# Fetching the sample's matrix-memory state one step sooner, into a third buffer

## The chip, the cores and the metric

The kernel runs on one core of a Trainium2 chip. The metric is the device time of one launch in microseconds (us), the median of several runs. TensorE (PE) does the matrix products, VectorE (DVE), ScalarE (ACT) and GpSimd (POOL) the work on elements, and SyncE (SP) issues most of the transfers (DMA). Each engine works through its own list of instructions in order; a semaphore makes one wait for another.

## The reference

One layer of a streaming encoder runs over 2048 prompt rows and 8 sample groups of 16 rows (128 rows in all), with a model width of 1024:

```python
h   = rms_norm(x)
z   = h @ w_in                               # q, k, v of attention and of the matrix memory, gates
A   = band_attention(...)                    # 8 heads x 64, own chunk and 8 chunks before it
B   = mlstm(...)                             # matrix memory, 4 heads x 128
x   = x + rms_norm(concat(rms_norm(A), sigmoid(o) * head_norm(B)) @ w_out)
x   = x + rms_norm(conv_ffn(rms_norm(x)))    # up, causal convolution of width 3, gated GELU, down
```

The change concerns `B` of the sample rows. Each of the 8 groups has a state of its own, C (128 x 128) and n (128) for each of the 4 heads, which is read, used and written back:

```python
num   = einsum('bhts,bhse->bhte', qk, v) + w_inter[..., None] * einsum('bhtd,bhde->bhte', q, c_prev)
c_new = decay[..., None, None] * c_prev + einsum('bhs,bhsd,bhse->bhde', w_s, k, v)
```

In the kernel n stands as one more column beside C, so a group's state of one head is 128 x 129 numbers.

## The kernel before, in words

All large products are split into three matmuls of rounded operands (high by high, high by low, low by high; lines 95 to 97). The program has two halves. First come the projections by `w_in`, in 28 groups of columns (14 for each half of the rows). Between their matmuls, two streams of small units are interleaved: the attention (`att_stream`) and the matrix memory (`mem_stream`). Each unit is a Python generator that stops (`yield`) with a cost for PE and DVE. After every piece of projection work `pump` (L171) steps one stream or the other while DVE's running cost is behind that of PE; one step (`Pipe.step`, L141) launches one new unit and advances all that are alive. Near the end of this part the output projection `project` (`w_out`, tiles `wo`, L956) takes the projection's place beside the last attention units; its units make their transposes in `mT_pt` from rows `mr`. When its first eight row tiles and the sample's are loaded, `open_ffn` gives the space of the first half to the FFN. There SP loads the normalised rows (`x2r`, L1061), ACT and POOL make their norm, DVE scales them (L1073), and PE transposes them (`h2T_pt`, L1081).

The pieces of one attention unit that matter here are the transposes `pt` of the weights, their rounding into `pth` (ACT, L399) and the rest `ptl` (DVE, L400), the product `ot` with the values (L412, L413), the copy `sh` of half of it (ACT, L418), and, at the end of a group, the transposes `ao`, scaled into `attst` (DVE, L430) and stored to memory (SP, L434).

For the sample rows `mlstm_sample(h)` (L716) yields `own` (the own products of the 16 rows), three empty units, four `batches(bp)` units of two groups each, and `finish`. A `batches` unit loads the states of two groups into `cs` (128 x 258, L763), builds the masked queries `qz` (POOL) and values `vz` (DVE), multiplies `qz` with `cs` and the keys with `vz` (tile `cus`, L775 and L776), updates `cs` (DVE, L779 and L780) and stores it (L781). `cs` shares its buffers (tag `num`) with the tile `num` of the prompt's chunks (L689), in which these collect their result and from which they store it (L649).

What stands in the lists of the engines in the end is set twice. The program text gives the order in which instructions are created, and the framework's scheduler then orders each engine's list by a cost model of its own, in which each instruction has an estimated time. An edit in one place can so change the order of all engines for a long stretch.

Of the kernel before, what the change touches and what calls it, by code (L numbers as in the profile page):

```python
# [10 lines left out]
F32 = mybir.dt.float32  # L11
# [6 lines left out]
P = 128  # L18
# [26 lines left out]
def hymba_step(ctx: ExitStack, tc: tile.TileContext, I: dict, O: dict):  # L45
    nc = tc.nc
# [13 lines left out]
    def ps_sm(name):  # L60
        return psum.tile([P, 512], F32, tag="sm", name=name)
# [4 lines left out]
    def transpose(out, in_, n=P):  # L66
        nc.tensor.transpose(out, in_, ident[:n, :n])
# [60 lines left out]
    pm = p1.enter_context(tc.tile_pool(name="pm", bufs=2))  # L128
# [33 lines left out]
    def bubble():  # L162
        return iter([])
# [319 lines left out]
    def load_gain(h, name):  # L483
        t = pm.tile([P, DH], F32, tag="hgm", name=f"hgm{name}", bufs=1)
        nc.sync.dma_start(t, I["g_mlstm"][0:1, h * DH:(h + 1) * DH].broadcast_to([P, DH]))
        nc.vector.tensor_scalar(t, t, 0.5, None, op0=ALU.mult)
        hgm[h] = t
# [163 lines left out]
    def mlstm(h, half):  # L651
        md, dec, cols = stab[half]
        e = DH + 1

        def load(s):
            sg, o = s.t0 // 4, s.t0 % 4
            s.mb = pm.tile([P, 2, P], F32, tag="mb", name=f"mb{s.nm}", bufs=2)
            nc.sync.dma_start(s.mb, md.rearrange("(c h) t -> h c t", c=8)[h:h + 1, 2 * s.pc:2 * s.pc + 2]
                              .broadcast_to([P, 2, P]))
            yield 0.0, 0.0  # L660
            s.qk = pm.tile([P, 2, 256], F32, tag="mqk", name=f"mqk{s.nm}", bufs=2)
            nc.sync.dma_start(s.qk, qkbd[h][sg][:, :, o * P:o * P + 256])
            vo = pm.tile([P, 2, 2 * DH + 1], F32, tag="mvo", name=f"mvo{s.nm}", bufs=2)
            s.va, s.og = vo[:, :, 0:e], vo[:, :, e:]
            nc.sync.dma_start(vo[:, :, 1:], vobd[h][sg][:, o:o + 2, :])
            nc.gpsimd.memset(vo[:, :, 0:1], 1.0)
            nc.gpsimd.affine_select(out=s.mb, in_=s.mb, pattern=[[0, 2], [1, P]], compare_op=ALU.is_ge, fill=BIG,
                                    base=0, channel_multiplier=-1)
            yield 0.0, 0.0
            if s.pc == 0:  # L670
                load_gain(h, f"{h}_{half}")
            yield 0.0, 0.0

        def chunk(s, c):
            cc = 2 * s.pc + c
            r = cc * HB + h
            col = lambda i: cols[:, i, r:r + 1]
            q_, k_ = s.qk[:, 0, c * P:(c + 1) * P], s.qk[:, 1, c * P:(c + 1) * P]
            sp = ps_sm(f"ms{s.nm}_{c}")
            nc.tensor.matmul(sp[:, 0:P], k_, q_, start=True, stop=True)  # L680
            transpose(sp[:, P:2 * P], k_)
            w = pm.tile([P, P], F32, tag="wexp", name=f"w{s.nm}_{c}", bufs=2)
            nc.scalar.activation(w, s.mb[:, c, :], AF.Exp, bias=col(0), scale=-1.0)
            kw = pm.tile([P, P], F32, tag="kw", name=f"kw{s.nm}_{c}", bufs=2)
            nc.scalar.activation(kw, sp[:, P:2 * P], AF.Identity, scale=col(3))
            nc.vector.tensor_tensor(w, sp[:, 0:P], w, op=ALU.mult)
            yield 0.32, 0.2
            if c == 0:
                s.num = pm.tile([P, 2, e], F32, tag="num", name=f"num{s.nm}", bufs=2)  # L689
            num = s.num  # L690
            acc = ps_sm(f"ma{s.nm}_{c}")
            nc.tensor.matmul(acc[:, e:2 * e], q_, cst[h], start=True, stop=True)
            nc.tensor.matmul(acc[:, 0:e], w, s.va[:, c, :], start=True, stop=True)
            nc.tensor.matmul(acc[:, 2 * e:3 * e], kw, s.va[:, c, :], start=True, stop=True)
            nc.vector.scalar_tensor_tensor(cst[h], cst[h], dec[:, cc, h:h + 1], acc[:, 2 * e:3 * e],
                                           op0=ALU.mult, op1=ALU.add)
            nc.scalar.activation(num[:, c, :], acc[:, e:2 * e], AF.Identity, scale=col(1))
            nc.vector.tensor_tensor(num[:, c, :], num[:, c, :], acc[:, 0:e], op=ALU.add)
            yield 0.65, 0.47
            if c == 0:  # L700
                return
            r0 = 2 * s.pc * HB + h
            sg, o = s.t0 // 4, s.t0 % 4
            finish_heads(num, cols[:, 2, r0:r0 + HB + 1:HB], s.og, h, 2,
                         mixd[sg][:, o:o + 2, 512 + h * DH:512 + (h + 1) * DH], s.nm)
            if half == 1 and s.pc == 3:
                nc.sync.dma_start(O["c_prompt"][h], cst[h])
            yield 0.0, 1.3

        pairs = [SimpleNamespace(pc=pc, t0=8 * half + 2 * pc, nm=f"{h}_{8 * half + 2 * pc}") for pc in range(4)]  # L710
        yield load(pairs[0])
        yield bubble()
        yield bubble()
        for s in pairs:
            if s.pc < 3:
                yield load(pairs[s.pc + 1])  # L716
            yield chunk(s, 0)
            yield chunk(s, 1)

    def mlstm_sample(h):  # L720
        md, dec, cols = stab["s"]
        e = DH + 1
        nm = f"s{h}"
        col = lambda i: cols[:, i, h:h + 1]
        s = SimpleNamespace()
# [31 lines left out]
            yield 0.2, 0.2  # L757

        def batches(bp):
            yield 0.0, 0.0  # L760
            bs = slice(2 * bp, 2 * bp + 2)
            cs = pm.tile([P, 2, e], F32, tag="num", name=f"cs{h}_{bp}", bufs=2)
            nc.sync.dma_start(cs, I["state_c"][h][:, bs])  # L763
            qz = pm.tile([P, 2, P], F32, tag="mqk", name=f"qz{h}_{bp}", bufs=2)
            nc.gpsimd.memset(qz, 0.0)
            for i in range(2):
                c = slice((2 * bp + i) * DS, (2 * bp + i + 1) * DS)
                nc.gpsimd.tensor_copy(qz[:, i, c], s.qt[:, c])
            vz = pm.tile([P, 2, e], F32, tag="mvo", name=f"vz{h}_{bp}", bufs=2)
            nc.vector.tensor_tensor(vz, s.va.unsqueeze(1).broadcast_to([P, 2, e]),  # L770
                                    ind[:, bs].unsqueeze(2).broadcast_to([P, 2, e]), op=ALU.mult)
            yield 0.0, 0.3
            cu = ps_sm(f"cu{nm}_{bp}")
            for i in range(2):
                nc.tensor.matmul(cu[:, 2 * e:3 * e], qz[:, i, :], cs[:, i, :], start=(i == 0), stop=(i == 1))  # L775
            nc.tensor.matmul(cu[:, :2 * e], s.kw, vz.rearrange("p b e -> p (b e)"), start=True, stop=True)  # L776
            nc.vector.scalar_tensor_tensor(s.num[:, 0, :], cu[:, 2 * e:3 * e], col(1), s.num[:, 0, :],
                                           op0=ALU.mult, op1=ALU.add)
            nc.vector.tensor_tensor(cs, cs, dec[:, h, bs].unsqueeze(2).broadcast_to([P, 2, e]), op=ALU.mult)  # L779
            nc.vector.tensor_tensor(cs, cs, cu[:, :2 * e].rearrange("p (b e) -> p b e", b=2), op=ALU.add)  # L780
            nc.sync.dma_start(O["c_sample"][h][:, bs], cs)  # L781
            yield 0.85, 0.8
# [11 lines left out]
        for bp in range(DB // 2):  # L794
            yield batches(bp)
# [390 lines left out]
    for n_, (half, gi) in enumerate(seq):  # L1186
        wh, wl, _ = pend
# [199 lines left out]
    for b, tiles in enumerate(FBLOCKS):  # L1387
# [74 lines left out]
        for f in range(NF):  # L1462
# [7 lines left out]
            e, c = ec[:, 0:512], ec[:, 512:1024]  # L1470
# [38 lines left out]
        for dh in range(2):  # L1509
# [57 lines left out]
            for j in order:  # L1567
                if dh == 0:
                    half, _, ssq = out[j]
# [3 lines left out]
                else:  # L1573
                    half, _, ssq = out[j]
# [104 lines left out]
```

## Time and profile before

| what | us |
|---|---|
| median of 3 runs (lowest and highest 2806.80, 2811.92) | 2807.41 |
| profiled execution, its own time | 2812.18 |
| span from the first to the last instruction of the profiled execution | 2810.5 |
| PE busy | 2729.8 (97%) |
| DVE busy | 1871.9 (67%) |
| ACT busy | 1407.5 (50%) |
| POOL busy | 446.2 (16%) |
| mean granted clock of PE | 0.997 |

The profile is one execution. In its views an instruction has its line, engine, operation, output and inputs (by the program's names, without numbers), and ahead of it in square brackets the time for which its engine was idle and what ended that. A list of waits has the total, the number of times and the longest. A window has the busy time of each engine with its number of instructions, the clock granted to PE (1.00 is full), the busy share of the transfer engines and the GB/s. The chain of waits follows what released each piece of work back in time.

### The profile page before, as it was taken

The numbers are of one execution on the slowest core, as the hardware profiler recorded it, in microseconds if no ns is written. First come the engines' busy times: TensorE is split into PE (matmuls) and PEld (weight loads), VectorE is DVE, ScalarE is ACT, GpSimd is POOL, SyncE is SP. The second block draws the span as 40 slices with busy tenths as digits, with TensorE's granted clock in tenths as the row PEclk, the third lists the DMA queues.
The fourth block names the chain that finished last, engine by engine and source line by source line (L and its number), as shares of the span: only waits on it lengthen the run. The fifth ranks groups of instructions, "written<-read, shape, count | busy, mean of one in ns | idle before, by whom it ended". The sixth has DMA issues, their size and how long they took to land.

```text
span 2810.5 us, 47049 instructions
## 1 busy us (share of the span) xinstructions
PE 2729.8 (97%) x16587; PEld 2550.2 (91%) x16587; DVE 1871.9 (67%) x3442; ACT 1407.5 (50%) x2836; POOL 446.2 (16%) x876
## 2 busy tenths in 40 slices
PE   8899999999999999999999999999999999999998
PEld 7899999998899998878999988799999878999887
DVE  5344455646446678666989886457878854888855
ACT  4345545644356666543545555445555543555533
POOL 1000010211100003244221110011111310222221
PEclk9999999999999999999999999999999999999999
DMA  4544355557555455355645455644544775555585
GB/s 164 170 128 125 111 155 156 177 148 215 164 173 148 141 177 172 106 180 203 199 160 173 162 177 172 218 145 154 157 154 139 266 264 155 171 181 175 188 298 197
DMA packets 313418, 486.04 MB, mean 173 GB/s; under 512 B 55426, under 2 KB 150622, under 8 KB 313054
## 3 DMA queue, kind: packets, MB, share of 16 engines
q1 hardware_dynamic: 274590, 449.21, 50.9%
q10 hardware_dynamic: 38592, 33.83, 3.6%
q8 instruction: 130, 2.13, 0.3%
q14 instruction: 106, 0.87, 0.1%
HBM read 359.36 MB, written 126.70 MB: 173 GB/s over the span
## 4 chain that ended last, share of the span: by engine, by line
PE 51%; DVE 5%; DMA 2%; issue 2%; ACT 1%; POOL 1%; SPq 0%; DVEq 0%; POOLq 0%; ACTq 0%
PE uec L95 5%; PE uec L96 5%; PE uec L97 5%; PE dn L96 4%; PE dn L97 4%; PE dn L95 4%; PE ua L97 3%; PE ua L96 3%; PE ua L95 3%; PE dnm L95 2%; PE dnm L97 2%; PE dnm L96 2%; PE wo L95 1%; PE wo L97 1%; PE wo L96 1%
## 5 line engine op out<-in xcount | busy, mean ns | idle before, releaser
L95 PE MATMUL uec<-B,wuh 128*128 128x384 f32 (+1 forms) x720 | 236.3, 329 | 6.9 <-DVE uu L1492 6.1
L96 PE MATMUL uec<-B,wuh 128*128 128x384 f32 (+1 forms) x720 | 235.2, 327 | 0.0
L97 PE MATMUL uec<-B,wul 128*128 128x384 f32 (+1 forms) x720 | 233.3, 327 | 0.0
L1251 DVE TENSOR_TENSOR gl<-gr,gh 128x768 fp32r<-128x768 f32 (+3 forms) x141 | 118.7, 849 | 163.3 <-ACT gh L1250 163.0
L1250 ACT CAST gh<-gr 128x768 fp32r<-128x768 f32 (+3 forms) x141 | 102.1, 736 | 219.1 <-PE dn L96 194.1
L1250 ACT CAST wuh<-wu 128x512 fp32r<-128x512 f32 x255 | 141.7, 617 | 91.2 <-PE uec L96 87.5
L95 PE MATMUL dn<-wdh,gh 128*128 128x512 f32 x466 | 182.9, 392 | 2.5 <-DVE ug L1403 2.5
L96 PE MATMUL dn<-wdl,gh 128*128 128x512 f32 x466 | 183.9, 395 | 0.0
L97 PE MATMUL dn<-wdh,gl 128*128 128x512 f32 x466 | 168.4, 396 | 0.0
L1251 DVE TENSOR_TENSOR wul<-wu,wuh 128x512 fp32r<-128x512 f32 x255 | 164.3, 683 | 2.8 <-DMA x2d<-mx 2.8
L96 PE MATMUL vo<-wi_l,hT 128*128 128x256 f32 x544 | 155.7, 286 | 0.0
L95 PE MATMUL vo<-wi_h,hT 128*128 128x256 f32 x544 | 154.9, 285 | 0.6 <-DVE mt L199 0.6
L97 PE MATMUL vo<-wi_h,hT 128*128 128x256 f32 x544 | 155.3, 285 | 0.0
L387 DVE CUSTOM_DVE_ANT_0 tmp<-s,nb 128x640 f32<-128x640 f32 (+4 forms) x128 | 94.3, 737 | 77.8 <-PE s L377 74.3
L95 PEld LDWEIGHTS uec<-B,wuh 128*128 128x128 f32 x720 | 135.1, 188 | 11.1 <-DVE uu L1492 8.1
L96 PEld LDWEIGHTS uec<-B,wuh 128*128 128x128 f32 x720 | 135.2, 188 | 0.1
L97 PEld LDWEIGHTS uec<-B,wul 128*128 128x128 f32 x720 | 135.0, 188 | 0.0
L388 ACT ACTIVATE tmp<-tmp,mn 128x640 f32<-128x640 f32 (+4 forms) x128 | 97.6, 762 | 69.9 <-DVE mn L387 65.6
L95 PE MATMUL qk<-hT,wi_h 128*128 128x384 f32 (+1 forms) x384 | 128.6, 335 | 3.5 <-ACT qk_st L226 1.7
L400 DVE TENSOR_TENSOR ptl<-pt,pth 128x640 fp32r<-128x640 f32 (+4 forms) x128 | 93.5, 737 | 55.4 <-ACT pth L399 54.4
L97 PE MATMUL qk<-hT,wi_l 128*128 128x384 f32 (+1 forms) x384 | 128.0, 333 | 0.0
L96 PE MATMUL qk<-hT,wi_h 128*128 128x384 f32 (+1 forms) x384 | 127.8, 333 | 0.0
(409 smaller groups left out, 8886.6 us busy)
## 6 DMA issues: line engine op xcount, KB each, us to landing
wu<-in_w_up SPq DMA_DIRECT2D x220, 256.0 KB, 4.0
wu<-wsd SPq DMA_DIRECT2D x176, 256.0 KB, 3.7
wdr<-in_w_down SPq DMA_DIRECT2D x132, 256.0 KB, 5.4
gr<-gd SPq DMA_DIRECT2D x78, 384.0 KB, 3.9
wi_raw<-in_w_in SPq DMA_DIRECT2D x52, 512.0 KB, 4.3
wsd<-ws SPq DMA_DIRECT2D x88, 256.0 KB, 4.0
gd<-g SPq DMA_DIRECT2D x44, 384.0 KB, 2.7
kraw<-kTd SPq DMA_DIRECT2D x112, 128.0 KB, 3.2
```

Of the source, the lines that this page charges most:

```text
L95: nc.tensor.matmul(out, ah, bh, start=start, stop=False, skip_group_check=onto)
L96: nc.tensor.matmul(out, ah, bl, start=False, stop=False, skip_group_check=onto)
L97: nc.tensor.matmul(out, al, bh, start=False, stop=stop, skip_group_check=onto)
L387: nc.vector.tensor_tensor_reduce(o_, s_, b_, 1.0, 3e38, ALU.add, ALU.min, accum_out=mn)
L388: nc.scalar.activation(tmp[:, :n], tmp[:, :n], AF.Exp, bias=mn, scale=-1.0, accum_out=rsum[:, i % 4, hh:hh + 1])
L400: nc.vector.tensor_tensor(s.ptl[:, sl, qc], ptv, s.pth[:, sl, qc], op=ALU.subtract)
L1250: nc.scalar.copy(h, r)
L1251: nc.vector.tensor_tensor(l, r, h, op=ALU.subtract)
```

## The change

The tag `num` has three buffers in place of two (in both places that use it, since the third is one of the tag), and in `batches` the tile `cs` is taken and its load issued ahead of the first `yield`, that is when the unit is launched, and no longer in the next step of the stream. The number of instructions that compute, store or load is the same, and so is what is computed. The third buffer takes 1032 bytes in each partition.

```diff
@@ -686,7 +686,7 @@
             if c == 0:
-                s.num = pm.tile([P, 2, e], F32, tag="num", name=f"num{s.nm}", bufs=2)
+                s.num = pm.tile([P, 2, e], F32, tag="num", name=f"num{s.nm}", bufs=3)
@@ -757,10 +757,10 @@
         def batches(bp):
+            bs = slice(2 * bp, 2 * bp + 2)
+            cs = pm.tile([P, 2, e], F32, tag="num", name=f"cs{h}_{bp}", bufs=3)
+            nc.sync.dma_start(cs, I["state_c"][h][:, bs])
             yield 0.0, 0.0
-            bs = slice(2 * bp, 2 * bp + 2)
-            cs = pm.tile([P, 2, e], F32, tag="num", name=f"cs{h}_{bp}", bufs=2)
-            nc.sync.dma_start(cs, I["state_c"][h][:, bs])
             qz = pm.tile([P, 2, P], F32, tag="mqk", name=f"qz{h}_{bp}", bufs=2)
```

The lists of all five engines differ from about 410 us to about 1230 us of the run before, and are alike ahead of and behind that. Three places show how. In the first, SP's list where the first head's states are loaded, `num_4` and `num_6` are the prompt's results in the same buffers, `mvos` the values of the sample rows, and the numbers behind `cs` are the unit and a running number. A row with + is of the change, one with - of the kernel before:

```order
 L319 DMA nb_0_4597<-relrow 128x640
+L762 DMA cs_0_4895<-in_state_c 128x258
 L649 DMA mixd_163<-num_4_4477 128x2x128
 L736 DMA mvos_4767<-vobd_4_146 128x256
-L763 DMA cs_0_4923<-in_state_c 128x258
+L762 DMA cs_1_4925<-in_state_c 128x258
 L485 DMA hgm_0_5398<-in_g_mlstm 128x128
 L649 DMA mixd_163<-num_6_4571 128x2x128
 L328 DMA qraw_0_4463<-qTd_0_109 64x512 x2
 L331 DMA kraw_0_0_4464<-kTd_0_90 64x512 x2
-L763 DMA cs_1_4974<-in_state_c 128x258
+L762 DMA cs_2_4968<-in_state_c 128x258
```

The first load moved ahead of the store of `num_4` (whose data is in another buffer now), and each of the next two stands where its predecessor stood. The second place is SP's list in the last head, the kernel before first:

```order
L649 DMA mixd_163<-num_6_7763 128x2x128
L763 DMA cs_1_8072<-in_state_c 128x258
L905 DMA atts_171<-so_8945 128x512
L891 DMA svr_1_9078<-in_cache_v 128x512
L891 DMA svr_2_9118<-in_cache_v 128x512
L781 DMA out_c_sample<-cs_0_8032 128x258
L763 DMA cs_2_8117<-in_state_c 128x258
L891 DMA svr_3_9140<-in_cache_v 128x512
L891 DMA svr_4_9167<-vs 16x512
L781 DMA out_c_sample<-cs_1_8072 128x258
L763 DMA cs_3_8164<-in_state_c 128x258
```

and with the change:

```order
L762 DMA cs_1_8034<-in_state_c 128x258
L1155 DMA wi_raw_8888<-in_w_in 128x1024
L485 DMA hgm_1_10431<-in_g_mlstm 128x128
L649 DMA mixd_163<-num_6_7763 128x2x128
L1155 DMA wi_raw_9116<-in_w_in 128x1024
L762 DMA cs_2_8066<-in_state_c 128x258
L781 DMA out_c_sample<-cs_0_8001 128x258
L762 DMA cs_3_8111<-in_state_c 128x258
```

`cs_2` no longer stands behind a store of `cs`; `cs_3` stands behind that of `cs_0` in place of that of `cs_1`. Loads of other streams (`svr`, the sample attention's cached values; `wi_raw`, projection weights) have changed places with them. The third place is the start of the FFN on PE: the last attention transposes `ao`, the output projection `wo` behind them, and the first FFN transposes `h2T_pt`, the kernel before first. Where the line of dots stands, 46 more `wo` matmuls follow, so that there are 51 of them:

```order
L67 MATMUL ao_3_15152<-ident,attT_3_14865 128x128 x2
L95 MATMUL wo_1_15191<-wo_13608,mt_14889 128x512
L96 MATMUL wo_1_15191<-wo_13608,mt_14889 128x512
L97 MATMUL wo_1_15191<-wo_13608,mt_14889 128x512
L95 MATMUL wo_0_15255<-wo_13395,mt_15099 128x512
...
L97 MATMUL wo_1_15332<-wo_13608,mt_15099 128x512
L1081 MATMUL h2T_pt_0_0_15268<-ident,x2r_15187 128x128 x4
```

and with the change, where the dots stand for 19 and there are 24:

```order
L67 MATMUL ao_3_15152<-ident,attT_3_14865 128x128 x2
L96 MATMUL wo_0_15255<-wo_13608,mt_15099 128x512
L97 MATMUL wo_0_15255<-wo_13608,mt_15099 128x512
L97 MATMUL wo_1_15332<-wo_13395,mt_15099 128x512
L95 MATMUL wo_1_15332<-wo_13395,mt_15099 128x512
...
L97 MATMUL wo_1_15332<-wo_13608,mt_15099 128x512
L1081 MATMUL h2T_pt_0_0_15268<-ident,x2r_15187 128x128 x4
L1081 MATMUL h2T_pt_1_0_15289<-ident,x2r_15189 128x128 x4
L1081 MATMUL h2T_pt_1_1_15316<-ident,x2r_15189 128x128 x4
L67 MATMUL mT_pt_15303<-ident,mr_15185 128x128 x8
L67 MATMUL mT_pt_15435<-ident,mr_15314 128x128 x8
```

27 of these `wo` now stand ahead of `ao`, and two groups of `mT_pt` stand together. On SP, `attst`, one load of a norm's gain and the loads of `x2r` follow each other in both kernels.

## The prediction

> **What bounds the kernel now.** I read the page first. Its busy line and its chain say which engine the end hangs on:
>
> ```profile
> span 2810.5 us, 47049 instructions
> PE 2729.8 (97%) x16587; PEld 2550.2 (91%) x16587; DVE 1871.9 (67%) x3442; ACT 1407.5 (50%) x2836; POOL 446.2 (16%) x876
> PE 51%; DVE 5%; DMA 2%; issue 2%; ACT 1%; POOL 1%; SPq 0%; DVEq 0%; POOLq 0%; ACTq 0%
> ```
>
> TensorE (PE) is busy for 97% of the span. The change adds and removes no matmul, so two things can move the time: the 2810.5 - 2729.8 = 80.7 us in which PE idles, and the clock that it is granted. Everything below is therefore a sum over PE's waits. The second view is the list of waits of PE; these are the rows that concern the stretch where the orders differ:
>
> ```profile
> PE cus L775 <- DMA cs<-in_state_c: 8.4, 6, 2.5
> PE mT_pt L67 <- DVE mr L979: 3.0, 1, 3.0
> PE pt L67 <- DVE ptl L400: 1.8, 1, 1.8
> PE h2T_pt L1081 <- DVE x2r L1073: 1.6, 1, 1.6
> ```
>
> The first row is the change's target: of the 16 groups of `cus` matmuls, 6 waited for the load of their state, 8.4 us in all, 2.5 us at most. The tile's own view and SyncE's (SP's) waits between 400 and 760 us show why the loads are late:
>
> ```profile
> L763 SPq DMA_DIRECT2D cs<-in_state_c x16: 327/332/520, 410.0 to 719.5; - x16
> SPq L763 <- DMA out_c_sample<-cs: 21.4, 7, 4.5
> SPq L763 <- DMA mixd<-num: 11.3, 7, 2.8
> ```
>
> The queue held 14 of the 16 loads back until a store out of the wanted buffer had landed: 7 times the store of an earlier `cs`, 7 times that of a `num`. One worst case, from the timeline, SP's and PE's rows:
>
> ```profile
> 703.87 0.61 PE L775 MATMUL cus<-cs,qz 128*128 128x129 f32 x4
> 709.74 0.34 SPq L781 DMA_DIRECT2D out_c_sample<-cs  x1
> 714.30 0.33 SPq L763 DMA_DIRECT2D cs<-in_state_c  x1
> 716.48 0.68 PE L775 MATMUL cus<-cs,qz 128*128 128x129 f32 x4 [2.46 <-DMA cs<-in_state_c]
> ```
>
> Unit 0 multiplies at 703.87, its result is stored at 709.74, the load into that buffer leaves at 714.30, unit 2 starts at 716.48. From `cus` of one unit to `cus` of the unit that inherits its buffer this chain takes 716.48 - 703.87 = 12.6 us.
>
> **The change, part by part.**
>
> *The waits that it removes: -8.4 us.* The load is issued one pump step sooner, and a third buffer makes that possible. By the order on SP, `cs_0` now stands ahead of the store of `num_4`, `cs_1` and `cs_2` each behind a `num` store, and only `cs_3` behind the store of `cs_0`; before, both `cs_2` and `cs_3` stood behind a `cs` store. A load lands within a few us of its issue (714.30 to 716.48 above is 2.2 us), and by the new order 24 to 28 matmuls lie between two units, 3.2 us or more at the shorter price worked out below, so I take units 0 to 2 as free. Bounds: 0 (nothing gained) to 8.4.
>
> *The clock that goes with the longest wait: -1.7 us.* Windows; the columns are the stretch, its length, busy time of PE, PEld, DVE, ACT, POOL, the granted clock, the DMA share and GB/s:
>
> ```profile
> 709.00:716.40 7.40, 4.67 (x32) 4.44 (x32) 3.51 (x10) 1.53 (x3) 0.64 (x3) 1.00 0.50 142
> 716.50:720.50 4.00, 4.00 (x19) 3.81 (x20) 2.35 (x10) 0.83 (x2) 0.64 (x3) 0.57 0.54 165
> 653.80:657.80 4.00, 3.97 (x33) 3.93 (x34) 2.47 (x11) 2.61 (x9) 0.88 (x4) 1.00 0.59 185
> ```
>
> Behind the wait of 2.46 us PE ran 4.0 us at 0.57, which is 4.0 x 0.43 = 1.7 us of lost work; behind the wait of 2.14 us at 653.8 it stayed at 1.00. If the long wait goes, so does this loss.
> [...]
>
> *What stays of the waits: +1.0 us.* `cs_3` still needs the chain of 12.6 us, from `cs_0`'s matmuls on. By the new order 93, 81, 80 and 74 matmuls lie between the two in the four heads (before, between 55 and 83 lay in such a chain). The price of one, from two windows:
>
> ```profile
> 590.00:600.00 10.00, 10.00 (x76) 10.00 (x75) 4.60 (x16) 4.74 (x16) 1.80 (x5) 1.00 0.53 160
> 703.00:712.00 9.00, 8.22 (x50) 7.45 (x51) 4.62 (x12) 1.16 (x2) 1.63 (x7) 1.00 0.61 180
> ```
>
> 10.00 / 76 = 0.132 us in the first, 8.22 / 50 = 0.164 in the second. At 0.164 they take 15.3, 13.3, 13.1 and 12.1 us: only the last falls short, by 0.5. At 0.132 they take 12.3, 10.7, 10.6 and 9.8, short by 0.3, 1.9, 2.0 and 2.8, which is 7.0. I take 1.0, near the first, because the stretches around `cus` are the ones that the second row measures; the ends are 0 and 7.0.
>
> *What the moved order costs at the end of the attention phase: +6.3 us.* The scheduler has put all engines in another order between some 410 and 1230 us. The memory units come 7 to 14 us of PE work sooner, the attention's last units up to 17 us later, the w_out projection (`wo`) 7 to 9 us sooner. That matters in one place. After the last attention transposes (`ao`), SP must store `attst` before it may load `x2r`, from which the FFN's first transposes (`h2T_pt`) are made. PE, SP, ACT and DVE in the timeline, the transfer from the chain of waits:
>
> ```profile
> 1207.18 0.38 PE L67 MATMUL ao<-ident,attT 128*128 128x128 f32 x2
> 1207.60 0.69 DVE L430 TENSOR_TENSOR attst<-ao,rinv 128x512 f32<-128x512 f32 x1 [1.91 <-PE ao L67]
> 1208.31 0.57 SPq L434 DMA_DIRECT2D mixd<-attst  x1
> 1210.08 7.15 DMA x2r<-x2d
> 1218.07 1.28 DVE L1073 SCALAR_TENSOR_TENSOR x2r<-x2r,n_rs,g 128x1024 f32<-128x1024 f32 x1 [3.45 <-POOL n_rs L84]
> 1219.51 0.63 PE L1081 MATMUL h2T_pt<-ident,x2r 128*128 128x128 f32 x4
> 1221.74 1.06 PE L1081 MATMUL h2T_pt<-ident,x2r 128*128 128x128 f32 x8 [1.61 <-DVE x2r L1073]
> ```
>
> `ao` to `h2T_pt` is 1219.51 - 1207.18 = 12.33 us, and the order on SP after `ao` is the same in both kernels. What covers it are `wo` matmuls:
>
> ```profile
> 1207.50:1219.50 12.00, 11.95 (x51) 9.27 (x50) 1.38 (x2) 0.00 (x0) 1.00 0.57 169
> ```
>
> (the same kind of window, of `wo` alone). 51 of them take 11.95 us, 0.234 each, and leave no wait and no slack. In the new order 24 stand there. The other 27, 27 x 0.234 = 6.3 us, were done earlier, and PE waits as long for `h2T_pt`: 12.33 - 0.38 - 24 x 0.234 = 6.3. The page's issues of transfers (KB of one, us to landing) bound it from below:
>
> ```profile
> x2r<-x2d SPq DMA_DIRECT2D x17, 512.0 KB, 3.9
> ```
>
> If 7.15 shrinks to 3.9, the hole is 6.3 - 3.2 = 3.1 us. From above I take 7.0, the 0.63 us of the first `h2T_pt` once more: after such a wait they may run at about half the clock. I expect that to cost 0, because the next wait (1.61 us, for DVE) covers it.
>
> *The transposes behind it: 0.* `mT_pt` of the next but one tile now stands directly behind that of the next one, where before some 30 `wo` lay between. DVE's rows there:
>
> ```profile
> 1221.51 1.28 DVE L1020 SCALAR_TENSOR_TENSOR mx<-mx,n_rs,norm_row 128x1024 f32<-128x1024 f32 x1
> 1222.71 0.68 DVE L1008 COPY mx<-wo 128x512 f32<-128x512 f32 x1
> 1223.31 2.49 DVE L979 TENSOR_SCALAR mr<-mr,att_rs 128x512 f32<-128x512 f32 x1
> 1231.84 0.48 DVE L979 TENSOR_SCALAR mr<-mr,att_rs 128x512 f32<-128x512 f32 x1
> ```
>
> The copy of 0.68 us is out of this chain now (its `wo` are done early), and L979 took 2.49 us once and 0.48 once; the second `mT_pt` adds one L1020, one L1094 (0.68) and one L979 to the path. If the first L979 becomes the short one, 1.5 us are gained; if both are long, 2.0 are lost. I take 0.
>
> *The transposes before it: +1.6 us.* The last pair of attention units now has no `wo` between the transposes `pt_15` and the product `ot_14`, where 23 stood. Then PE waits for the cast on ACT (L399), the copy ahead of it in ACT's queue (L418) and DVE's difference (L400):
>
> ```profile
> L399 ACT CAST pth<-pt 128x640 fp32r<-128x640 f32 x96 | 65.5, 692 | 41.1 <-PE pt L67 29.1 <-PE ot L412 7.9 <-DMA qkbd<-qb_st 2.1
> L418 ACT COPY sh<-ot 64x256 f32<-64x256 f32 x64 | 23.6, 369 | 40.2 <-PE ot L413 38.8 <-ACT va_st L224 0.4
> L400 DVE TENSOR_TENSOR ptl<-pt,pth 128x640 fp32r<-128x640 f32 (+4 forms) x128 | 93.5, 737 | 55.4 <-ACT pth L399 54.4
> ```
>
> Two casts and the copy are 2 x 0.69 + 0.37 = 1.75, of which a little lies under `pt_15` itself; the wait of 1.8 us on `ptl` in the list above is the same pattern. Bounds 0.7 (one cast) to 2.5 (two casts, the copy and a difference of 0.74).
>
> *Other waits in the reordered stretch: 0.* PE idled
>
> ```profile
> 760.00:1060.00 300.00, 298.89 (x2281) 293.64 (x2279) 184.34 (x419) 185.10 (x443) 19.44 (x61) 1.00 0.56 166
> 1060.00:1207.00 147.00, 143.21 (x840) 123.43 (x841) 108.86 (x213) 80.74 (x207) 44.19 (x65) 1.00 0.42 128
> ```
>
> 1.1 us and 3.8 us in these stages. They can vanish at best, so -4.9, and I allow as much on the other side.
>
> The sum: -8.4 - 1.7 + 1.0 + 6.3 + 0 + 1.6 + 0 = -1.2 us. The profiled execution took 2812.18 us, 1.7 more than its span, so it would be 2811.0. It lies 4.8 us above the median of the runs shown (2807.41), so the forecast for the median is 2806.2. I count less than 0.2% (5.6 us) as no change, since a measurement of this kernel can hardly tell less; -1.2 is the same.
>
> **The rivals.**
>
> *The hole stays small, and the gain stays.* The 27 `wo` are not lost: they stand where PE idled 3.8 us, and if they fill that and the `x2r` loads take 3.9 us, the terms are -8.4 - 1.7 + 1.0 + 3.1 + 1.6 - 3.8 = -8.2: 2799.2. For it: 7.15 us is the landing of several loads at once, in a busy stretch. Against it: SP's rows after `ao` are unchanged, and so is what is in flight there.
>
> *The wait moves to `cs_3`.* It is slower than before. Place: the fourth unit of each head, behind the store of the first. Price: 7.0 in place of 1.0, and 1.7 of clock, once, for the wait of 2.8. It decides from the point where PE takes less than 12.6 / 80 = 0.158 us for a matmul between the two. -1.2 + 6.0 + 1.7 = +6.5: 2813.9. For it: the window at 590 has 0.132. Against it: the one at 703 has 0.164.
>
> *The change doesn't do what it says.* SP is one queue; `cs_0` now stands behind the loads of the attention's caches, and if SP is late at them the load lands no sooner. Then the 8.4 and 1.7 stay and only the moved order counts: +6.3 + 1.6 = +7.9: 2815.3. For it: SP waited 21.4 + 11.3 us at these loads. Against it: those waits were for buffers, of which there is one more.
>
> **How the numbers follow.** Forecast (same) 0.50, gain with a small hole 0.25, wait at `cs_3` 0.15, no earlier load 0.10. The terms left open put 0.03 of the forecast's half beyond 5.6 us on either side; the fast rival ends faster in nine tenths of its cases (0.23), the two slow ones slower in eight tenths (0.20). That gives faster 0.26, slower 0.23, same 0.51. The range leaves out a tenth at either end: from 2798, just under the fast rival's value, to 2816, just above the slowest. The forecast's own range is 2802 to 2812: 4 below, if the hole stays at 3.1 and a wait in the tail is filled, 6 above, if `cs_3` costs its 7.0.
>
> **What would show it.** Right: no `cus` wait on a load beyond the fourth unit of a head, clock 1.00 in that stretch; PE waits some 6 us for `x2r` ahead of the first `h2T_pt`, with 24 `wo` after `ao`; a wait on `ptl` or `pth` before the last `ot`. Wrong: `cus` waits still of several us (second or third rival), a wait of under 4 us for `h2T_pt` (first), or a new PE wait of over 3 us between 760 and 1200 us that none of the terms names.

## The result and the profile after

The change is slower. Its median is 2834.39 us (2832.77 to 2835.34, 4 runs) against 2809.66 us for the kernel before (2806.8 to 2814.83, 4 runs): a ratio of 1.0089, with a 95% interval of 1.0075 to 1.0102. The forecast was no change, 2806.2 us in a range from 2798 to 2816. The page of the change (profiled execution 2832.77 us):

```profile
span 2831.0 us, 47052 instructions
PE 2739.9 (97%) x16587; PEld 2556.9 (90%) x16587; DVE 1873.2 (66%) x3442; ACT 1408.3 (50%) x2836; POOL 444.3 (16%) x876
```

The span grew by 20.5 us. Half of that, 91.1 - 80.7 = 10.4 us, is idle time of PE; the other half, 10.1 us, is PE working longer at the same 16587 matmuls. The list of PE's waits says that the change's target was met, and what grew:

```profile
PE mT_pt L67 <- DVE mr L979: 10.3, 6, 4.6
PE h2T_pt L1081 <- DVE x2r L1073: 7.4, 2, 6.2
PE ss L95 <- ACT skh L846: 4.0, 2, 3.1
PE wo L95 <- ACT wo L946: 2.1, 1, 2.1
PE cus L776 <- DVE vz L770: 1.9, 1, 1.9
PE cus L775 <- DMA cs<-in_state_c: 1.5, 1, 1.5
PE ot L412 <- ACT pth L399: 1.3, 1, 1.3
```

`cus` waited 8.4 us for its loads before and waits 1.5 now; `mT_pt` went from 3.0 to 10.3 and `h2T_pt` from 1.6 to 7.4. Where in the program that lies is best seen in windows between the same instructions of both kernels. The five stages are: from 152 us, where both kernels are alike, over the sample's memory to the first `qb` matmul of the second half of the rows (757.4 us before); from there to the first `wo`; to the last `ao`; to the first `h2T_pt`; to the first FFN up-projection. The columns are as in the prediction's windows. Before:

```profile
152.00:757.40 605.40, 586.61 (x4156) 568.75 (x4155) 319.02 (x815) 296.52 (x723) 62.11 (x190) 1.00 0.51 153
757.40:1055.50 298.10, 297.05 (x2274) 292.82 (x2273) 181.97 (x414) 182.23 (x438) 18.22 (x58) 1.00 0.55 162
1055.50:1207.20 151.70, 147.85 (x865) 126.95 (x864) 113.30 (x221) 85.24 (x218) 45.41 (x67) 1.00 0.44 135
1207.20:1219.50 12.30, 12.25 (x54) 9.60 (x53) 3.45 (x5) 4.36 (x10) 1.79 (x4) 1.00 0.58 175
1219.50:1329.10 109.60, 104.37 (x496) 84.78 (x497) 75.46 (x75) 41.72 (x87) 52.55 (x62) 0.98 0.58 193
```

and with the change:

```profile
151.40:757.30 605.90, 587.73 (x4156) 570.11 (x4155) 318.94 (x815) 295.81 (x723) 60.54 (x190) 0.99 0.50 153
757.30:1048.70 291.40, 290.57 (x2216) 286.35 (x2215) 170.74 (x385) 173.24 (x412) 15.18 (x51) 1.00 0.52 157
1048.70:1226.10 177.40, 166.89 (x950) 141.71 (x949) 124.87 (x251) 96.25 (x245) 47.22 (x75) 0.98 0.41 131
1226.10:1238.30 12.20, 6.00 (x27) 4.54 (x25) 3.37 (x5) 4.64 (x11) 1.73 (x4) 0.89 0.42 150
1238.30:1351.50 113.20, 106.29 (x496) 86.81 (x497) 74.41 (x72) 41.09 (x85) 52.44 (x63) 0.94 0.56 187
```

The second number of a row is its length, the third PE's busy time, and their difference the idle time. Three things are to be seen.

- In the first stage, the one that the change is about, nothing was gained: 18.8 us idle before, 18.2 after, although the waits on the loads are gone.
- In the second stage 58 matmuls fewer are done (2216 for 2274), and in the third 85 more (950 for 865). The attention's and memory's units have slid from the second stage into the third, and 27 `wo` have come into it from the fourth.
- The third stage has 10.5 us idle where it had 3.9, the fourth 6.2 for 0.05, the fifth 6.9 for 5.2. (Outside the five stages, where the lists are alike, PE idled 3.2 us less in this execution, so that the sum is 10.4.) In the third stage 8.3 of the 10.5 us are waits of the output projection itself: `mT_pt` for its rows `mr` 4.9, in four waits, and `wo` for the cast of its weights (ACT, L946) 2.1 and for its rows `mt` 1.3. In the old order these were 0.4 there, and the longest wait was 1.8, of `pt` for `ptl`.

Most of the rest is the clock. Four stretches of the change at half clock, by windows:

```profile
740.70:747.50 6.80, 6.80 (x22) 5.27 (x21) 2.89 (x5) 2.10 (x5) 1.23 (x2) 0.50 0.51 175
1058.20:1061.60 3.40, 3.40 (x11) 2.61 (x10) 3.40 (x9) 3.40 (x8) 0.00 (x0) 0.50 0.84 300
1146.90:1150.30 3.40, 3.40 (x16) 3.36 (x16) 3.08 (x10) 3.13 (x9) 0.19 (x1) 0.50 0.59 231
1235.70:1252.70 17.00, 7.82 (x33) 6.66 (x34) 13.52 (x11) 7.53 (x15) 12.36 (x14) 0.50 0.48 154
```

By the granted 0.50 I put half of the busy time in them, (6.8 + 3.4 + 3.4 + 7.8) / 2 = 10.7 us, as lost; in the kernel before the same sum between 400 and 1300 us is 3.2 (3.4 us at 717.1 and 3.0 busy at 1225.7, both at 0.50). That is an estimate, and a little high: in the change's trace `wo` matmuls of one shape start 0.43 us apart at 0.50 (from 1058.58 to 1060.71) and 0.23 at 1.00 (from 1227.04 to 1230.31). By the estimate 7.5 us of the 10.1 are clock. The other 2.6 us stay unplaced.

The end of the attention phase, PE's timeline in the change:

```profile
1226.12 0.38 PE L67 MATMUL ao<-ident,attT 128*128 128x128 f32 x2
1238.33 1.12 PE L1081 MATMUL h2T_pt<-ident,x2r 128*128 128x128 f32 x4 [6.23 <-DVE x2r L1073]
1240.66 1.94 PE L1081 MATMUL h2T_pt<-ident,x2r 128*128 128x128 f32 x8 [1.21 <-DVE x2r L1073]
1243.32 1.97 PE L67 MATMUL mT_pt<-ident,mr 128*128 128x128 f32 x8 [0.71 <-DVE mr L979]
1249.90 1.97 PE L67 MATMUL mT_pt<-ident,mr 128*128 128x128 f32 x8 [4.62 <-DVE mr L979]
```

The hole ahead of `h2T_pt` is there and is 6.23 us long, 12.21 after `ao`. But the last `ao` itself is already 18.9 us later than before (1226.12 for 1207.18), of which 27 x 0.234 = 6.3 are the `wo` done ahead of it. So some 12.6 us were lost before this place, for which the prediction had 1.6 us of transposes and otherwise nothing. The wait of 4.62 us for the second `mT_pt` is long because DVE's two instructions ahead of it took 5.4 us, and both ran beside POOL's two additions (timeline, DVE and POOL):

```profile
1244.53 2.83 DVE L1094 TENSOR_TENSOR B<-b,B 128x512 fp32r<-128x512 f32 x1
1247.29 2.56 DVE L979 TENSOR_SCALAR mr<-mr,att_rs 128x512 f32<-128x512 f32 x1
1243.74 5.82 POOL L1021 TENSOR_TENSOR mx<-mx 128x1024 f32<-128x1024 f32 x2
```

L1094 took 0.68 us and L979 0.48 where no such addition ran (the change at 1254.62 and 1011.73). In the traces of the kernel before and of the change, L979 took 0.47 to 0.49 us in all 8 cases without one of these additions (L1021) beside it, and 2.49 to 2.65 in 25 of the 26 with one.

### The profile page after: what moved, and what is told of

Read it like the earlier page. It is cut to its first block, busy times and chain, and to the rows that moved or that the text cites. A ratio compares the mean times of both kernels' runs of the same rounds, so it can differ in the third digit from the quotient of the medians.

```text
span 2831.0 us, 47052 instructions
## 1 busy us (share of the span) xinstructions
PE 2739.9 (97%) x16587; PEld 2556.9 (90%) x16587; DVE 1873.2 (66%) x3442; ACT 1408.3 (50%) x2836; POOL 444.3 (16%) x876
## 4 chain that ended last, share of the span: by engine, by line
PE 76%; DMA 10%; DVE 7%; ACT 3%; issue 3%; POOL 1%; SPq 0%; ACTq 0%; DVEq 0%; POOLq 0%
PE uec L95 5%; PE uec L96 5%; PE uec L97 5%; PE dn L96 4%; PE dn L97 4%; PE dn L95 4%; PE ua L97 3%; PE ua L96 3%; PE ua L95 2%; PE dnm L95 2%; PE dnm L97 2%; PE dnm L96 2%; PE qb L97 2%; PE qb L95 2%; PE qb L96 2%
## 5 line engine op out<-in xcount | busy, mean ns | idle before, releaser
L95 PEld LDWEIGHTS uec<-B,wuh 128*128 128x128 f32 x720 | 135.3, 188 | 10.5 <-DVE uu L1492 7.0
```

The source lines that it names most:

```text
L95: nc.tensor.matmul(out, ah, bh, start=start, stop=False, skip_group_check=onto)
```

## The experiments

All ratios are to the kernel before, run on the same chip beside them. Theory A says that the third buffer makes the scheduler put the engines in another order, and that this order costs the time. Theory B says that fetching sooner, or a third buffer as such, costs it, whatever the order.

**The load alone.** The load ahead of the first `yield`, but with two buffers (the diff is to the change):

```diff
-                s.num = pm.tile([P, 2, e], F32, tag="num", name=f"num{s.nm}", bufs=3)
+                s.num = pm.tile([P, 2, e], F32, tag="num", name=f"num{s.nm}", bufs=2)
-            cs = pm.tile([P, 2, e], F32, tag="num", name=f"cs{h}_{bp}", bufs=3)
+            cs = pm.tile([P, 2, e], F32, tag="num", name=f"cs{h}_{bp}", bufs=2)
```

> The load issued ahead of the first yield as in the change, but with two buffers. The lists of all five engines come out in the order of the kernel before. Theory A (the third buffer lets the scheduler put the engines in another order, and that order costs the time; the earlier place of the load in the text does nothing by itself): ratio to before 1.000, within 0.2%. Theory B (fetching sooner collides with other transfers or blocks SP, whatever the order): slower, towards 1.009.

Measured: 0.9998 (0.9987 to 1.0008; 2809.66 us). Moving the load in the text does nothing: with two buffers the scheduler puts it where it stood. Since the lists are those of the kernel before, this run is also a second look at it, and two of its numbers matter: the `cus` waits on loads were 3.4 us (3 of them) in place of 8.4 (6), and the first stage, the sample's, had 604.1 - 589.4 = 14.7 us idle in place of 18.8:

```profile
150.30:754.40 604.10, 589.38 (x4156) 571.08 (x4156) 319.55 (x815) 296.02 (x723) 64.01 (x190) 0.99 0.50 153
```

**The buffer alone.** Three buffers in both places, the load where it was:

```diff
-            cs = pm.tile([P, 2, e], F32, tag="num", name=f"cs{h}_{bp}", bufs=2)
+            cs = pm.tile([P, 2, e], F32, tag="num", name=f"cs{h}_{bp}", bufs=3)
```

(and the same for `num`; the diff is to the kernel before.)

> Three buffers, the load where it was. The lists come out in the order of the change. Theory A: as the change, 1.009 (1.007 to 1.011). Theory B, if the step sooner is what costs: 1.000; if it is the third buffer as such, 1.009 too, which the kernel with a third buffer and the old tail (x02) then tells apart.

Measured: 1.0068 (1.0051 to 1.0084; 2829.16 us), which overlaps the change's 1.0075 to 1.0102. Its waits are the change's; the last row is its sample stage:

```profile
PE mT_pt L67 <- DVE mr L979: 10.6, 6, 4.6
PE h2T_pt L1081 <- DVE x2r L1073: 6.9, 2, 5.7
PE cus L775 <- DMA cs<-in_state_c: 0.3, 1, 0.3
150.50:752.90 602.40, 588.10 (x4156) 570.55 (x4156) 318.97 (x815) 296.21 (x723) 60.44 (x190) 0.99 0.51 154
```

So of the two edits the buffer is the whole change. Its sample stage had 602.4 - 588.1 = 14.3 us idle, as much as the 14.7 of the run before, though `cus` waited 0.3 us in place of 3.4. Three kernels further down have the change's lists in this stage too, and they had 14.6, 17.1 and 17.4 us. So one order's idle time differs by some 4 us from one execution to the next (14.7 and 18.8 with the old order, 14.3 to 18.2 with the new one), and a gain of 8.4 isn't among these numbers.

**A third buffer with the old order behind it.**

```diff
-            cs = pm.tile([P, 2, e], F32, tag="num", name=f"cs{h}_{bp}", bufs=2)
+            cs = pm.tile([P, 2, e], F32, tag="csx" if bp in (0, 2) else "num", name=f"cs{h}_{bp}", bufs=1 if bp in (0, 2) else 2)
```

> cs_0 and cs_2 share one buffer of their own, cs_1, cs_3 and num keep the two of num: three buffers in all. Only cs_2 still waits for a store of cs (that of cs_0). The engines' order differs from before up to some 725 us and is the old one from there: 51 wo behind the last ao. Theory A: the cus waits fall from 8.4 to 2 to 4 us and nothing is lost later: 0.998 (0.9965 to 1.000), no wait of 6 us for h2T_pt. Theory B (a third buffer or an earlier load costs as such): slower by 0.3% or more.

Measured: 1.0000 (0.9991 to 1.0010; 2810.98 us). Theory B falls: a third buffer with earlier loads is there, and nothing is lost. But the gain that A expected isn't there either. The `cus` wait fell to 2.0 us as expected, and the sample stage had 604.2 - 589.5 = 14.7 us idle, like the repeat of the old order:

```profile
152.70:756.90 604.20, 589.50 (x4156) 571.10 (x4155) 318.81 (x815) 296.06 (x723) 61.78 (x190) 0.99 0.51 153
```

**One buffer given to one unit.** The same edit with `bp in (1,)`, and in a second kernel with `bp in (3,)`:

> Two buffers of num as before, and one buffer of its own for cs_1 of every head; the load where it was. cs_1 is fetched a head ahead, cs_0, cs_2 and cs_3 as late as before. PE's order is that of the change (apart from a few transposes at the start), with 24 wo behind the last ao. Theory A (the order costs the time): as the change, 1.007 to 1.009, with the same waits at mT_pt and h2T_pt. Theory B (a third buffer or an earlier load costs as such): as the next kernel, since both give one buffer to one unit.

> The same with the buffer given to cs_3 in place of cs_1. PE's order is that of before from some 725 us on, with 51 wo behind the last ao. Theory A: 1.000 (0.998 to 1.001), waits at mT_pt and h2T_pt as before. Theory B: as the kernel with a buffer for cs_1.

Measured: 1.0099 (1.0083 to 1.0115; 2835.18 us) with the buffer for `cs_1`, and 1.0016 (1.0005 to 1.0027; 2812.18 us) with the buffer for `cs_3`. The two give the same memory to one unit each and fetch one unit early; they differ in the order that the scheduler made of it. The waits, `cs_1` first:

```profile
PE mT_pt L67 <- DVE mr L979: 9.3, 6, 4.6
PE h2T_pt L1081 <- DVE x2r L1073: 7.2, 2, 6.0
```

```profile
PE mT_pt L67 <- DVE mr L979: 3.0, 1, 3.0
PE h2T_pt L1081 <- DVE x2r L1073: 1.2, 1, 1.2
```

This is theory A's case. The second is slightly above the bound given (1.001).

**Only the hole undone.** The change, with the sample tile's `wo` bound behind the last `ao` (`last_ao` holds that instruction; the bond is one of issue order on PE):

```diff
-                    mm3(acc, s.mt[:, 0, k, :], s.mt[:, 1, k, :], wo[k][0][:, c], wo[k][1][:, c],
-                        start=(k == 0), stop=(k == KT - 1))
+                    with tc.issue_after(last_ao[0].ins) if t == SAMPLE else ExitStack():
+                        mm3(acc, s.mt[:, 0, k, :], s.mt[:, 1, k, :], wo[k][0][:, c], wo[k][1][:, c],
+                            start=(k == 0), stop=(k == KT - 1))
```

> The change, with the 48 wo matmuls of the sample's row tile bound to be issued behind the last ao. PE's order differs from the change in 13 rows, so all is as in the change but the hole. If the hole before h2T_pt and the half clock behind it are the whole loss: back to before or below, 0.997 to 1.000. If they are a part, as the change's trace says (wait 6.2 to about 1, second mT_pt wait 4.6 to 0, clock 2.4 us): 10 us less than the change, 1.005, and the waits between 1050 and 1226 us stay. If the order at that place doesn't matter: 1.009.

Measured: 1.0053 (1.0039 to 1.0068; 2826.54 us), as expected for "a part". Third, fourth and fifth stage of it:

```profile
1047.40:1219.50 172.10, 160.13 (x929) 135.91 (x927) 125.07 (x251) 96.25 (x245) 47.19 (x75) 0.99 0.43 135
1219.50:1231.60 12.10, 11.46 (x51) 8.92 (x49) 2.77 (x4) 2.66 (x5) 0.93 (x3) 1.00 0.50 156
1231.60:1343.90 112.30, 107.13 (x496) 86.85 (x497) 73.26 (x75) 42.76 (x91) 51.49 (x63) 0.95 0.56 189
```

The hole is closed (12.1 - 11.5 = 0.6 us idle), and the third stage still has 12.0 us of idle time. The hole is less than half of the loss.

**The third stage: memory units beside `wo`?** One wait of the change, in its chain of waits, suggested a cause:

```profile
1135.66 3.76 DMA mb<-md
1139.48 0.41 POOL mb L667
1139.89 0.69 POOL mf L641
1140.60 0.62 DVE num L647 x2
1141.21 1.20 DVE mx L1020
1143.15 2.59 DVE mr L979
1145.79 0.66 PE mT_pt L67 x4
```

POOL waits for the load of a memory unit (`mb`), DVE behind it makes that unit's end (`num`) and only then the row norm `mr`, and PE's `mT_pt` comes last. In the order before, the last memory units are further on when `wo` begins. So on top of the hole's bond, each `wo` of the first eight row tiles was bound behind the memory matmuls ahead of it in the text (`last_ms` holds the last of these):

```diff
-                    with tc.issue_after(last_ao[0].ins) if t == SAMPLE else ExitStack():
+                    with tc.issue_after(last_ao[0].ins) if t == SAMPLE else tc.issue_after(last_ms[0].ins) if t < 8 else ExitStack():
```

> The change, with the sample tile's wo behind the last ao as in the kernel with 48 wo there, and besides each wo of the prompt's first eight row tiles bound to be issued behind the memory matmuls that are ahead of it in the program text, so that the last memory units no longer stand beside wo. If the waits between 1050 and 1226 us (idle of PE 10 to 12 us there, 3.6 to 3.9 in the old order) come from the memory's work on POOL and DVE getting in the way of the row norms: idle there falls to some 5 us, and the time to some 1.002 to 1.003. If they come from the crowding of the attention's tail alone: no change against 1.005.

Measured: 1.0105 (1.0089 to 1.0122; 2837.23 us): slower, and neither expectation came in. Its second and third stage:

```profile
757.50:1086.00 328.50, 311.96 (x2323) 304.12 (x2322) 194.67 (x443) 195.53 (x466) 18.95 (x61) 0.98 0.51 155
1086.00:1236.40 150.40, 143.86 (x820) 122.58 (x818) 100.40 (x192) 71.61 (x189) 43.56 (x64) 1.00 0.38 117
```

The idle time of the third stage fell to 6.5 us, near the 5 foreseen, but the second now has 16.5, most of it in waits of attention units behind the last projection matmul (`s` for `ptl` 4.1 us, `pt` for `mn` 3.2). I read this as: the streams' units wait wherever they stand without projection work between them, and moving `wo` moves the place. So the question was no longer what is beside `wo`, but why units that needed filler were left over when the projection ended.

**The projection held behind the streams.** From the lists of PE one can count how many projection and `wo` matmuls stand ahead of the first matmul of a unit (`s4_8` is the scores of attention head 4, row tile 8; `ms3_8` memory head 3):

| unit | before | change | projection held |
|---|---|---|---|
| `s0_8` | 3636 | +0 | +0 |
| `s2_8` | 4048 | +20 | +5 |
| `s3_12` | 4367 | +29 | +1 |
| `s4_8` | 4456 | +50 | +8 |
| `s4_12` | 4637 | +91 | +19 |
| `s5_12` | 4752 | +69 | 0 |
| `ms3_8` | 4848 | +63 | 0 |
| last `ao` | 5112 | +24 | 0 |

In the second half of the rows the change lets the projection run ahead of the streams, by up to 91 matmuls. The last experiment takes that back and leaves all else of the change, its loads and its order up to some 800 us, as it is. A table names, for 41 tiles of the projection and of `wo` from `s0_8` on, the scores that stand ahead of them in the old order:

```diff
+    HELD = {
+        "vo0_1_12": "s0_9", "vo0_1_14": "s0_10", "vo0_1_15": "s0_11", "qb1_1_0_1": "s1_9", "qb1_1_0_2":
...
+        "s6_11", "wo3_0": "s7_9", "wo4_0": "s7_11", "wo7_0": "s7_15"
+    }
+
+    def held(name):
+        ctx_ = ExitStack()
+        for n in HELD.get(name, "").split():
+            ctx_.enter_context(tc.issue_after(mark[n].ins))
+        return ctx_
...
+                    with held(f"{name}_{t}") if k == 0 else ExitStack():
```

(the last line around the first product of each tile, in the places where projections are made; `mark` holds a matmul of each unit's scores. The sample's `wo` stay bound behind the last `ao`.)

> The change, with the projection's and the output projection's matmuls of the second half bound behind the attention scores that stand ahead of them in the order of before (41 such bonds; the sample's wo behind the last ao). In the change the attention's and memory's units of the second half fall behind the projection by 20 projection matmuls at the second pair, 50 at the fourth, 90 at the fifth, and still 50 to 70 when w_out begins; here by 0 to 25 and then 0. The first 800 us keep the change's order and its early loads. Theory A as it stands now (the loss is that the streams fall behind, so that 70 matmuls which fill waits are used up before the attention's tail): ratio 0.998 to 1.001, idle of PE between the first wo and the last ao back from 10 to 4 us, h2T_pt without the wait of 6 us, half clock as in the old order. If the loss comes from the third buffer, the earlier loads or the order of the first 800 us: 1.005 or more stays.

Measured: 1.0014 (1.0002 to 1.0025; 2813.49 us), a little over the bound of 1.001. The five stages:

```profile
151.60:759.40 607.80, 590.45 (x4157) 572.05 (x4156) 319.48 (x815) 296.21 (x723) 60.58 (x190) 0.99 0.50 153
759.40:1057.80 298.40, 296.65 (x2275) 292.66 (x2273) 182.93 (x414) 184.02 (x440) 19.19 (x57) 1.00 0.53 162
1057.80:1209.80 152.00, 147.73 (x864) 127.09 (x864) 112.67 (x222) 84.51 (x215) 45.32 (x68) 1.00 0.42 134
1209.80:1221.80 12.00, 12.00 (x55) 9.62 (x53) 3.46 (x5) 4.33 (x10) 2.24 (x6) 1.00 0.51 184
1221.80:1330.80 109.00, 104.16 (x498) 84.75 (x497) 75.42 (x75) 41.72 (x87) 52.39 (x61) 0.98 0.58 194
```

From the second stage on they are the stages of the kernel before (298.4, 152.0, 12.0 and 109.0 us for 298.1, 151.7, 12.3 and 109.6). So the loss of 0.9% is the order of the second half, nearly all of it, and neither the buffer nor the loads. The third stage agrees over all kernels: it idled 10.4 to 12.0 us in the four that have the change's order there, and 3.3 to 4.3 in the five that have the old one. What is shown is that this order costs it. That the cost arises because filler (projection matmuls that stand between units that wait) is used up too early is how the table, the stages and the run with `wo` behind the memory fit together; no run measures it by itself. A second reading isn't excluded: about half of the third stage's idle time is waits for row norms, and the units that slid in bring DVE and POOL work that may hold these up. Why the scheduler lets the projection ahead when a tile of an earlier stage has one buffer more wasn't tried: that a buffer for `cs_1` does it and one for `cs_3` doesn't shows only that it hangs on small things. No kernel here beat the one before beyond its interval.

## Why the prediction was wrong, step by step

- **The waits removed, -8.4, and what stays, +1.0.** The waits did go (to 1.5, and 0.3 with the buffer alone). The 1.5 fell on a third unit, which was put at nothing. The first step that failed is the one from a wait that is gone to time that is gained. The stage's idle time went from 18.8 to 18.2 us, and from 14.7 to 14.3 in the second pair of runs. Other waits took the place: `ss` on `skh` 1.9 to 4.0 us, `cus` on `vz` 0 to 1.9. Besides, 8.4 was one draw: the same lists gave 3.4 in the next run.
- **The clock of the longest wait, -1.7.** It wasn't gained: a new wait of 3.1 us on `skh` at 739.8 was followed by 6.8 us at half clock (3.4 lost), for 3.4 us before (1.7 lost). The lists of the kernel before, run again with the load alone, had 10.2 us at 0.50 in this stage (637.3 to 647.5). Two executions of one order differ by more than the term, so it was no term that belongs to an order.
- **The wait that moves to `cs_3`** did not happen: no load of a `cs_3` was waited for. From the first to the fourth unit of a head, 15.3, 14.2, 12.4 and 15.1 us passed, for a chain put at 12.6. SP's list was read rightly.
- **The hole, +6.3.** Measured 6.23, 5.7 and 6.0 in three kernels with this order: mechanism and size were right. But its clock, put at 0, wasn't: 7.8 us of work fell into half clock behind the hole for 3.0 before, 2.4 us more.
- **The transposes behind it, 0.** Wrong by 2.3 us: `mT_pt` waited 0.71 and 4.62 for 3.04. The bound given was 2.0. The second L979 and an L1094 took 2.56 and 2.83 us beside POOL's additions, where I had taken 0.68 for L1094.
- **The transposes before it, +1.6.** Measured 1.26.
- **Other waits in the reordered stretch, 0 with 4.9 on either side.** This is the step that failed most: 8.7 us were put at 0. Idle time from the first `wo` to the last `ao` grew by 6.6 us (1.3 of which is the step above), and two stretches of half clock there cost 3.4 more (1.7 to 3.4 in the four kernels with this order, 0 to 1.7 in the five with the old one). I had the fact in hand ("the attention's last units up to 17 us later") and said that it "matters in one place". The count of matmuls by stage, 58 out of a stage that had hardly any idle time and 85 into one that had, could have been made from the lists beforehand.
- **The premise.** Idle time and clock were to be all that can move the time. By the estimate of half the busy time at 0.50 they were 17.9 of the 20.5 us; the other 2.6, which PE took more for the same matmuls, stay unplaced.
- **The rivals.** None of the three came in as written: the hole didn't stay small, no wait moved to `cs_3`, and the loads did land sooner. "The change doesn't do what it says" came nearest, since both gains are missing from the sum, but not for its reason, a late SP.

## What to carry to other kernels

When a list scheduler makes the order, an edit has to be judged by the whole order that it brings, not by the wait at which it is aimed: count, per stage, how much waiting work and how much filler each engine gets before and after. A wait that is removed in a stretch where several streams wait for each other can come back under another name, as here, so its price is the fall of the stage's idle time, and that wants two looks at the old kernel. If an edit is wanted without its new order, bind the few instructions that matter to their old neighbours in issue order, as the last experiment did with 41 bonds; here that took back the loss (1.0089 to 1.0014), and there was no gain to keep.

## What the runs showed of the hardware

Half clock here is a stretch for which the profile has a granted clock of 0.50. In the traces of the kernel before and of the change every such stretch, but for the last one of each, which ends with the program (6.4 and 6.8 us), lasted 3.41 us or a whole multiple of it. The kernel before had 3.41 us at 95.9, 717.1, 1225.7 and 2669.5; the change had 3.41 us at 95.6, 1058.2, 1146.9 and 2689.7, 6.83 at 740.7 and 17.07 at 1235.7. Within each trace the starts lie a whole number of 3.413 us apart: in the change those at 740.7, 1058.2, 1146.9 and 1235.7 are 93, 26 and 26 times that apart. Counted from the start of the span, this grid lies at 0.30 us in the kernel before and at 0.03 in the change.

By its length alone a wait of PE doesn't say whether half clock followed. In the two traces (but for the first 20 and the last 12 us of each) it set in within 3.4 us of the end of none of the 33 waits of 0.9 to 1.8 us, of 2 of the 9 of 1.8 to 2.2 us, and of 5 of the 6 of 2.2 to 3.4 us. With the traces cut into windows of 3.413 us on their grids, the cases come apart: all 10 windows at 1.00 in which PE idled 2.09 us or more were followed by one at 0.50, and none of the 729 in which it idled 1.83 us or less (none lay between). The wait of 2.14 us that ended at 653.83 in the kernel before is split by the grid at 652.25 into 0.56 and 1.58 us, and the clock stayed at 1.00; that of 2.09 us that ended at 1145.79 in the change lies in one window, and 3.41 us at 0.50 followed from 1146.9. So in these two traces a wait near 2 us was followed by 3.41 us at 0.50 (1.7 us of work lost, by the estimate above) or by none, as it lay on the grid. That is a count and no threshold: over all ten traces, cut in the same way, all 49 windows at 1.00 with 1.85 us or more were followed by 0.50, but so were 7 of the 30 with 1.6 to 1.85 us and 6 of the 2908 with less. No run moved a wait on the grid, and why the clock falls is not shown.

The lists of the kernel before had 3.4 us at 0.50 in the sample stage in one execution (717.1) and 10.2 in the next (637.3 to 647.5, with the load alone), a loss of 1.7 and 5.1 us by the same estimate. The loads of the state were waited for 8.4 us in the first and 3.4 in the second, with the same lists on all engines.
